# Head products of the second block: from two passes of 128 rows to three passes of 64 rows, two heads by turns

## The chip, the cores and the metric

The kernel runs on one core of a Trainium2 chip, in one launch. The metric is the device time of one execution in microseconds (us), the median of several runs; lower is better. Each core has five engines with instruction streams of their own: PE (TensorE) multiplies matrices, DVE (VectorE) and ACT (ScalarE) work element by element, POOL (GpSimd) does odd jobs, and SP issues most of the transfers. The profile shows PE in two rows: PE for the products themselves, and PEld for the loads of the stationary operand that go ahead of each product.

## What is computed

Two networks run one behind the other on 512 tokens of 1024 channels. Block 1 is a mixer of four branches and a mixture of experts. Block 2, where the change lies, is two layers, each with a token mixer of 16 heads of 64 channels and an MLP:

```python
HEAD_DIM = 64
RET_HEADS = 4      # retention: rotated q and k, decay by distance, chunks of 128
DSA_HEADS = 4      # attention over keys that an index chose
DIL_HEADS = 8      # dilated attention
IDX_HEADS = 8      # heads of the index, 64 channels each; the best keys by their weighted relu scores
...
inner = jnp.einsum('bhncd,bhnmd->bhncm', qc, kc) * decay[None, :, None]
```

All four use products of queries and keys over the 64 channels of one head, which this text calls head products. Float32 accuracy is wanted, and the kernel makes it from parts: a float32 value is split into a high part in the engine's one-pass format (fp32r) and the low part that is left over, and a product of two values is the sum of the products of their parts.

## The kernel before

Everything is traced by `Net`. Its work is written as threads (generators) that yield the engine on which they go on and what they wait for; `run` picks, by a rough clock of the engines (`Clock`), the thread that can start first, and each engine then runs its instructions in the order in which they were picked. No order is written out by hand. `Clock.cost` prices a product by its columns alone.

The activations lie as 128 channels by 512 tokens. `jobs_block2` lists the projections of a layer, and `stream` runs them with their weights loaded ahead; `chan` is one of them: 8 chunks of the contraction in three products each (`mm3`: high by high, high by low, low by high), 512 columns wide. `v_job` makes values, 256 columns wide. While the projections run, the units of the heads are mixed between them: `ret_head` (retention), `idx_unit` (the index), `causal_unit` (the masked attentions of both kinds). Each takes a bank of PSUM (`bank` in the trace, 8 of them, 512 columns each), makes its head product into it, and hands it to DVE or ACT.

A pair of heads comes out of a projection as 128 rows: the first head's 64 channels, then the second's. The kernel before rearranges these for each head, in tiles of the ring `G` (10 tiles of 128 x 1024):

- `stack` puts a head's query parts on top of each other: 64 rows of high parts, 64 rows of low parts. It takes one copy on ACT and one subtraction on DVE, of 64 rows each.
- `dup` writes a head's key parts in both halves of the rows: a copy and a subtraction, and two further copies on ACT or DVE, whichever the clock finds less busy.

With that a head product is two passes over all 128 rows: the stacked queries by the doubled high parts of the keys, then by the doubled low parts. In the code this is the loop `for z in range(2)` in each unit. The three tiles of a pair of heads (`qk_tiles`) are the stacked queries, the keys' high parts and the keys' low parts.

A unit's products are 256, 384 or 512 columns wide (never under 256: narrower ones are made wider). `attend` keeps a number of units under way: 3 of retention, 6 of the masked attentions. In the trace all instructions carry one line, L320, since a helper issues them, so groups go by tiles: `G,G` are the head products, `g_hi`, `g_lo` the activations, `whi`, `wlo` the parts of the weights, `mt` the ring of scratch tiles, `vr` the values, `cP` and `cT` the probabilities and their transposes.

Of the kernel before, what the change touches and what calls it, by code (L numbers as in the profile page):

```python
# [27 lines left out]
F32R = mybir.dt.float32r  # L28
I32 = mybir.dt.int32
AF = mybir.ActivationFunctionType  # L30
OP = mybir.AluOpType
# [171 lines left out]
def _span(ap):  # L203
    """the tile of an access pattern, and the range of its elements on a partition"""
    pairs = ap.ap
    row = pairs[0][0]
    lo = ap.offset % row if row > 0 else ap.offset
    hi = lo
    for s, n in pairs[1:]:
        d = s * (n - 1)  # L210
        if d < 0:
            lo += d
        else:
            hi += d
    return ap.tensor.name, lo, hi + 1


class Clock:
# [91 lines left out]
class Lane:  # L310
    """an engine, with what is traced on it noted on the clock"""
# [26 lines left out]
class Ring:  # L338
    """tiles that are taken and given back in any order"""
# [28 lines left out]
class Net:  # L368
    """The kernel. What it does is written as threads (generators), which yield the engine that their next
    instructions run on and what those wait for; `run` traces them in the order of a rough clock's times, the first  # L370
    in time first. Each engine runs its instructions in the order in which they are traced."""
# [199 lines left out]
    def proj(self, out, w, act, kt, n):  # L571
        """out[128 channels, n tokens] = the weights' columns by the activations"""
# [5 lines left out]
    def proj_t(self, out, w, act, t):  # L578
        """out[128 tokens of tile t, 256 channels]; w: the two halves of the contraction"""
# [7 lines left out]
    def split(self, hi, lo, src, *free):  # L587
        """hi + lo = src; then the rings' tiles in `free` are given back"""
# [7 lines left out]
    def evacuate(self, out, p, n):  # L596
        """a bank's first n columns into out"""
# [8 lines left out]
    def evacuated(self, ring, p, n):  # L606
        """a bank's first n columns, in a tile of the ring"""
# [8 lines left out]
    def rsqrt_mean(self, out, sums, n):  # L616
        """out = (sums / n + eps) ** -0.5"""
# [6 lines left out]
    def row_bcast(self, out_sb, colv, nt):  # L624
        """out_sb[128, nt * 128] = the [128 tokens, nt] column values, along the tokens on every row"""
# [8 lines left out]
    def square(self, acc, x, sq, first, scaled=None):  # L634
        """acc (+)= x ** 2, by a tile of the ring sq; scaled: also (f * x) ** 2, by f and its square"""
# [15 lines left out]
    def column_sums(self, r, acc, nt, n):  # L651
        """r[128 tokens, nt] = (mean over n channels of the squares in acc + eps) ** -0.5"""
# [7 lines left out]
    def sumsq(self, p, nt, k, x, sq):  # L660
        """columns of p: the sums over the 128 channels of chunk k of x ** 2, by tokens"""
# [9 lines left out]
    def rms(self, r, p, nt, nk):  # L671
        """r[128 tokens, nt] = (mean over the chunks' channels + eps) ** -0.5; the bank p is given back"""
# [6 lines left out]
    def square_last(self, x, sq, event):  # L679
        """a tile of the ring sq with x ** 2"""  # L680
# [25 lines left out]
    def silu_c(self):  # L706
        """silu(c) and silu(c_ctx), and their parts"""
# [26 lines left out]
    def mod_job(self, g, kq, w):  # L734
        """rows of the bank: the parts of c by the weights' columns"""
# [35 lines left out]
    def modulated(self, pool, x, nt, v, hi, lo, name):  # L771
        """hi + lo = x / rms * A + B"""
# [34 lines left out]
    def modulation_rest(self, ws, accs):  # L807
        """g1, sh2, sc2, g2: the two 128-column groups of each unit"""
# [45 lines left out]
    def merge(self, n, a, done=0):  # L854
        """some gates ahead of their branches (the first ones may have been done before)"""
# [25 lines left out]
    def branch_job(self, n, d, w):  # L881
        """acc (+)= 2 sigmoid(gate) * (y @ w), by sigmoid(g) = (tanh(g / 2) + 1) / 2"""
# [116 lines left out]
    # -- convolution  # L999
# [10 lines left out]
    def conv_first(self, *ws):  # L1010
        """some units at once, by parts of the contraction"""
# [21 lines left out]
    def conv_tail(self, c, half, p):  # L1033
        """z = a * sigmoid(b), by sigmoid(b) = (tanh(b / 2) + 1) / 2"""
# [29 lines left out]
    def conv_norm(self):  # L1064
        """silu(rms norm), by silu(v) = (tanh(v / 2) + 1) * v / 2"""
# [25 lines left out]
    # -- Fourier  # L1091
# [35 lines left out]
    def dft(self, g, f):  # L1127
        """y = Re(DFT over tokens and channels): the channels' DFT, then its cosines' less its sines' over the tokens"""
# [44 lines left out]
    # -- neighbourhood attention  # L1173
# [3 lines left out]
    def scratch(self, es):  # L1177
        """rows in DRAM: the values of the neighbourhoods, the experts' input by tokens, and their output by blocks"""
# [5 lines left out]
    def zeros(self):  # L1184
        """a row of zeros after the experts' output"""
# [28 lines left out]
    def pair_ring(self, pool, n, shape, name):  # L1214
        """a ring of tiles for high parts, and the tiles of their low parts by the names of those"""
# [48 lines left out]
    def na_values(self):  # L1264
        """for each pair of heads, the values of the four windows of columns and of the context"""
# [64 lines left out]
    def dup(self, hi, lo, src, rows):  # L1330
        """hi, lo [128, n]: the parts of src's 64 rows, in both halves of the partitions"""
# [1844 lines left out]
```

## Time and profile before

| what | value |
|---|---|
| median of 3 runs | 2463.21 us (2459.06 to 2466.94) |
| span of the profiled execution, first to last instruction | 2460.7 us |
| PE busy in it | 2395.9 us, 97% |
| DVE busy, ACT busy | 1675.1 us, 1236.0 us |
| token mixer of block 2, first layer | about 1160 to 1420 us |
| token mixer of block 2, second layer | about 1800 to 2060 us |

The profile gives the span alone for the profiled execution, no time around it. The span is 2.5 us under the median and inside the range of the runs. In the timeline a product's duration runs from its start to the modelled end of its pipeline, so consecutive products overlap: what a product costs its engine is the distance from its start to the next start, called its slot here, and not its duration. Rows of one group that follow each other are merged, with xN behind them; a merged row of N products divided by N gives the slot, if it is taken to the start of the row behind it.

### The profile page before, as it was taken

The numbers are of one execution on the slowest core, as the hardware profiler recorded it, in microseconds if no ns is written. First come the engines' busy times: TensorE is split into PE (matmuls) and PEld (weight loads), VectorE is DVE, ScalarE is ACT, GpSimd is POOL, SyncE is SP. The second block draws the span as 40 slices with busy tenths as digits, with TensorE's granted clock in tenths as the row PEclk, the third lists the DMA queues.
The fourth block names the chain that finished last, engine by engine and source line by source line (L and its number), as shares of the span: only waits on it lengthen the run. The fifth ranks groups of instructions, "written<-read, shape, count | busy, mean of one in ns | idle before, by whom it ended". The sixth has DMA issues, their size and how long they took to land.

```text
span 2460.7 us, 33539 instructions
## 1 busy us (share of the span) xinstructions
PE 2395.9 (97%) x12332; PEld 2011.6 (82%) x12332; DVE 1675.1 (68%) x3144; ACT 1236.0 (50%) x2135; POOL 160.3 (7%) x179
## 2 busy tenths in 40 slices
PE   7999999999997999999999999999999999999998
PEld 3789788889886788887889888888888888888886
DVE  6997577788455989898998753444569976533443
ACT  4433466468342777775537743332443665432333
POOL 3100122100001110002000000000000000000000
PEclk9999999999997999999999999999999999999999
DMA  6223443521363998985121132222232112222221
GB/s 251 97 69 107 134 128 111 170 77 44 99 213 113 351 384 325 353 325 182 64 78 53 44 103 94 94 97 101 95 101 78 53 64 72 95 100 95 94 98 57
DMA packets 104907, 323.79 MB, mean 132 GB/s; under 512 B 12850, under 2 KB 19922, under 8 KB 104612
## 3 DMA queue, kind: packets, MB, share of 16 engines
q1 hardware_dynamic: 91284, 285.40, 33.0%
q0 software_dynamic: 8560, 25.01, 3.5%
q10 hardware_dynamic: 4896, 11.22, 1.2%
q8 instruction: 98, 1.61, 0.3%
q14 instruction: 69, 0.57, 0.1%
HBM read 308.45 MB, written 13.11 MB: 131 GB/s over the span
## 4 chain that ended last, share of the span: by engine, by line
PE 38%; issue 14%; DVE 1%; DMA 0%; ACT 0%; ACTq 0%; POOLq 0%; POOL 0%; DVEq 0%
PE bank L320 38%; DMA mraw<-yg,dest 0%; DVE wlo L320 0%; DVE G L320 0%; DVE cP L320 0%; DVE ym L320 0%; DVE mt L320 0%; DVE m L320 0%; ACTq L320 0%; DVE x L320 0%; DVE o L320 0%; ACT whi L320 0%; POOLq L3172 0%; POOL r L320 0%; DVE nm L320 0%
## 5 line engine op out<-in xcount | busy, mean ns | idle before, releaser
L320 ACT CAST whi<-wraw 128x1024 fp32r<-128x1024 f32 (+1 forms) x321 | 322.1, 1006 | 666.8 <-PE bank L320 633.2
L320 DVE TENSOR_TENSOR wlo<-wraw,whi 128x1024 fp32r<-128x1024 f32 (+1 forms) x321 | 375.4, 1173 | 155.6 <-ACT whi L320 154.8
L320 PE MATMUL bank<-g_hi,whi 128*128 128x512 f32 x992 | 395.9, 399 | 0.0
L320 PE MATMUL bank<-g_hi,wlo 128*128 128x512 f32 x992 | 387.3, 390 | 0.2
L320 PE MATMUL bank<-g_lo,whi 128*128 128x512 f32 x992 | 386.5, 390 | 0.0
L320 PEld LDWEIGHTS bank<-g_hi,wlo 128*128 128x128 f32 x992 | 186.2, 188 | 40.9 <-DVE wlo L320 1.1
L320 PE MATMUL bank<-h_hi,whi 128*128 128x512 f32 x528 | 216.9, 411 | 1.5 <-ACT whi L320 1.5
L320 PEld LDWEIGHTS bank<-g_hi,whi 128*128 128x128 f32 x992 | 186.5, 188 | 37.9 <-issue 1.9
L320 PEld LDWEIGHTS bank<-g_lo,whi 128*128 128x128 f32 x992 | 186.5, 188 | 37.1 <-issue 1.9
L320 PE MATMUL bank<-h_hi,wlo 128*128 128x512 f32 x528 | 209.3, 396 | 1.3 <-DVE wlo L320 1.3
L320 PE MATMUL bank<-h_lo,whi 128*128 128x512 f32 x528 | 208.6, 395 | 1.6 <-DVE h_lo L320 1.6
L320 PE MATMUL bank<-u_hi,whi 128*128 128x512 f32 x512 | 202.4, 395 | 0.0
L320 PE MATMUL bank<-u_hi,wlo 128*128 128x512 f32 x512 | 200.7, 392 | 0.0
L320 PE MATMUL bank<-u_lo,whi 128*128 128x512 f32 x512 | 198.8, 388 | 0.0
L320 DVE SCALAR_TENSOR_TENSOR mu<-bank,rbc 128x512 f32<-128x512 f32 x64 | 44.0, 691 | 161.0 <-PE bank L320 157.4
L320 ACT CAST whi<-mraw 128x1024 fp32r<-128x1024 f32 x101 | 105.7, 1050 | 55.0 <-PE bank L320 25.1
L320 DVE TENSOR_TENSOR wlo<-mraw,whi 128x1024 fp32r<-128x1024 f32 x101 | 121.0, 1218 | 16.5 <-ACT whi L320 14.5
L320 PEld LDWEIGHTS bank<-h_hi,wlo 128*128 128x128 f32 x528 | 100.6, 191 | 24.5 <-DVE wlo L320 2.5
L320 PEld LDWEIGHTS bank<-h_hi,whi 128*128 128x128 f32 x528 | 101.0, 191 | 21.3 <-ACT whi L320 1.9
L320 PEld LDWEIGHTS bank<-h_lo,whi 128*128 128x128 f32 x528 | 100.9, 191 | 19.5 <-DVE h_lo L320 2.1
L320 PEld LDWEIGHTS bank<-u_hi,wlo 128*128 128x128 f32 x512 | 96.1, 188 | 22.5
L320 PEld LDWEIGHTS bank<-u_lo,whi 128*128 128x128 f32 x512 | 96.1, 188 | 21.2
(539 smaller groups left out, 5017.7 us busy)
## 6 DMA issues: line engine op xcount, KB each, us to landing
mraw<-in_wgu SPq DMA_DIRECT2D x106, 512.0 KB
wraw<-in_win SPq DMA_DIRECT2D x102, 512.0 KB
wraw<-in_wdn SPq DMA_DIRECT2D x78, 512.0 KB
wraw<-in_wup SPq DMA_DIRECT2D x64, 512.0 KB
mraw<-in_wdn SPq DMA_DIRECT2D x50, 512.0 KB
mw<-in_wmod SPq DMA_DIRECT2D x64, 256.0 KB
wraw<-in_wout SPq DMA_DIRECT2D x24, 512.0 KB
wraw<-in_wgu SPq DMA_DIRECT2D x22, 512.0 KB
```

The source lines that it names most:

```text
L320: r = f(*args, **kw)
```

## The change

`put_qk` splits the 128 rows of a pair of heads as they are (`split`: one copy on ACT, one subtraction on DVE, all 128 rows), for queries and keys alike, so `stack` and `dup` are no longer called for them; `dup` stays for the index's keys. A pair of heads holds two tiles of `G` in place of three, and the ring has 9 tiles in place of 10. A head product is then three passes of 64 rows (high by high, high by low, low by high), and `head_products` makes those of a pair of heads by turns: first head, second head, in each pass. The first head's operands lie in rows 0 to 63, the second's in rows 64 to 127, and each head has a bank of its own. The units become units of pairs: `ret_pair`, `idx_pair`, `causal_pair`, each of which takes two banks at once; `attend` keeps 2 and 3 of them under way.

```diff
-        self.G = self.ring(pool, 10, [128, 1024], F32R, "G")
+        self.G = self.ring(pool, 9, [128, 1024], F32R, "G")
...
-        self.attend([self.ret_head(L, c, i) for c in range(2) for i in range(2)], 3)
-        u = [self.causal_unit(L, "l", hd, qt) for hd in range(8) for qt in range(4)]
-        u[24:24] = [self.causal_unit(L, "s", hd, qt) for hd in range(4) for qt in range(4)]
-        self.attend(u, 6)
+        self.attend([self.ret_pair(L, c) for c in range(2)], 2)
+        u = [self.causal_pair(L, "l", c, qt) for c in range(4) for qt in range(4)]
+        u[12:12] = [self.causal_pair(L, "s", c, qt) for c in range(2) for qt in range(4)]
+        self.attend(u, 3)
...
-            t = [self.G.take() for _ in range(3)]
+            t = [self.G.take() for _ in range(2)]
...
     def put_qk(self, tiles, j, t):
-        for i in range(2):
-            if j == 0:
-                yield from self.stack(tiles[0][:, i], t, 64 * i)
-            else:
-                yield from self.dup(tiles[1][:, i], tiles[2][:, i], t, 64 * i)
+        yield from self.split(tiles[j][:, 0], tiles[j][:, 1], t)
+
+    def head_products(self, outs, a, b):
+        for z, (y, x) in enumerate(((0, 0), (0, 1), (1, 0))):
+            for i in range(2):
+                r = slice(64 * i, 64 * i + 64)
+                self.nc.tensor.matmul(outs[i], a[y][r], b[x][r], start=z == 0, stop=z == 2)
...
-    def causal_unit(self, L, kind, hd, qt):
+    def causal_pair(self, L, kind, c, qt):
+        nn = max(128 * (qt + 1), 256)
+        yield PE, f"{kind}{L}{c}", (self.banks, 2)
+        q, k = self.D[kind, c][0]
+        ss = [self.banks.take() for _ in range(2)]
+        self.head_products([s[:, :nn] for s in ss], [q[:, z, qt * 128:(qt + 1) * 128] for z in range(2)],
+                           [k[:, z, :nn] for z in range(2)])
+        self.used((kind, c), 4)
+        for i in range(2):
+            self.spawn(self.causal_unit(L, kind, 2 * c + i, qt, ss[i]), 0, "head")
+        yield PE, f"head{L}{kind}{2 * c}{qt}", f"head{L}{kind}{2 * c + 1}{qt}"
+
+    def causal_unit(self, L, kind, hd, qt, s):
```

`ret_pair` and `idx_pair` are changed in the same way.

How PE's instructions stand is shown at two places. The first is in the retention of the first layer of block 2, between the last projections of its gates; `mt,vr` are the retention's products with the values. Before:

```order
L320 MATMUL bank_73<-mt_9636,vr_9646 128x384
L320 MATMUL bank_69<-mt_9637,vr_9646 128x256
L320 MATMUL bank_71<-G_9634,G_9635 128x256
L320 MATMUL bank_71<-G_9634,G_9626 128x256
L320 MATMUL bank_67<-G_9634,G_9635 128x256
L320 MATMUL bank_67<-G_9634,G_9626 128x256
L320 MATMUL bank_66<-g_hi,whi_103 128x512
L320 MATMUL bank_66<-g_lo,whi_103 128x512
```

Now:

```order
L320 MATMUL bank_69<-mt_9636,vr_9645 128x256
L320 MATMUL bank_66<-G_9633,G_9634 128x256
L320 MATMUL bank_68<-G_9633,G_9634 128x256
L320 MATMUL bank_66<-G_9633,G_9634 128x256
L320 MATMUL bank_68<-G_9633,G_9634 128x256
L320 MATMUL bank_66<-G_9633,G_9634 128x256
L320 MATMUL bank_68<-G_9633,G_9634 128x256
L320 MATMUL bank_73<-g_hi,whi_103 128x512
```

Two heads' products were four of 128 rows, a bank after the other; they are six of 64 rows, the banks by turns, with products of 128 rows on both sides. The rows shown (128x256) are those of the output, which stay.

The second place is near the end of the first layer's mixer, in the masked attentions, where transposes (`ident,cP`) and products with the values (`cT,vr`) stand around the head products. Before:

```order
L320 MATMUL bank_66<-cT_9645,vr_9649 128x128 x2
L320 MATMUL bank_67<-G_9630,G_9632 128x256
L320 MATMUL bank_67<-G_9631,G_9632 128x256
L320 MATMUL bank_70<-G_9630,G_9632 128x384
L320 MATMUL bank_70<-G_9631,G_9632 128x384
L320 MATMUL bank_68<-G_9630,G_9632 128x512
L320 MATMUL bank_68<-G_9631,G_9632 128x512
L320 MATMUL bank_73<-ident,cP_9640 128x128 x3
```

Now:

```order
L320 MATMUL bank_66<-cT_9644,vr_9647 128x128 x2
L320 MATMUL bank_70<-G_9631,G_9630 128x512
L320 MATMUL bank_68<-G_9631,G_9630 128x512
L320 MATMUL bank_70<-G_9631,G_9630 128x512
L320 MATMUL bank_68<-G_9631,G_9630 128x512
L320 MATMUL bank_70<-G_9631,G_9630 128x512
L320 MATMUL bank_68<-G_9631,G_9630 128x512
L320 MATMUL bank_69<-ident,cP_9639 128x128 x3
```

Units of three different sizes stood together; now it is one size of one pair. Over both layers there were 352 head products in 79 unbroken runs; there are 528 in 50 runs, 34 of them of one pair (six products), 14 of three pairs, one of four and one of eight.

## Rows read from the trace of the kernel before

**Rows 1.** The page: PE's busy time, and the granted clock in 40 slices.

```profile
PE 2395.9 (97%) x12332; PEld 2011.6 (82%) x12332; DVE 1675.1 (68%) x3144; ACT 1236.0 (50%) x2135; POOL 160.3 (7%) x179
...
PEclk9999999999997999999999999999999999999999
```

**Rows 2.** Busy time by engine in block 2's two token mixers (stretch: length, busy).

```profile
1160.00:1420.00 260.00, 259.12 (x1520) 223.56 (x1519) 227.80 (x593) 156.34 (x327) 7.10 (x6) 1.00 0.19 63
...
1800.00:2060.00 260.00, 259.19 (x1513) 223.10 (x1512) 215.60 (x570) 152.31 (x321) 9.90 (x10) 1.00 0.21 68
```

**Rows 3.** PE's waits from 1160 to 1420 us (waiter, awaited: total us, times).

```profile
PE bank L320 <- DVE cT L320: 0.5, 1, 0.5
PE bank L320 <- DVE mt L320: 0.2, 1, 0.2
```

**Rows 4.** Head products by width, both layers (count, busy us, mean ns, idle).

```profile
L320 PE MATMUL bank<-G,G 128*128 128x256 f32 x160 | 31.7, 304 | 0.0
L320 PE MATMUL bank<-G,G 128*128 128x512 f32 x96 | 29.8, 398 | 0.0
L320 PE MATMUL bank<-G,G 128*128 128x384 f32 x96 | 28.8, 381 | 0.1
```

**Rows 5.** Timeline of PE (start, duration): products 256, 384 and 512 wide.

```profile
1187.37 0.40 PE L320 MATMUL bank<-G,G 128*128 128x256 f32 x2
1187.61 0.29 PE L320 MATMUL bank<-whi,g_hi 128*128 128x256 f32 x1
...
507.05 0.33 PE L320 MATMUL bank<-kd_lo,qs 128*128 128x384 f32 x1
507.22 0.33 PE L320 MATMUL bank<-kd_hi,qs 128*128 128x384 f32 x1
...
1199.27 0.62 PE L320 MATMUL bank<-G,G 128*128 128x512 f32 x2
1199.73 0.28 PE L320 MATMUL bank<-whi,g_hi 128*128 128x256 f32 x1
```

**Rows 6.** Loads of PEld by group: eight at a time, 128 rows and 4 rows.

```profile
L320 PEld LDWEIGHTS bank<-ones,rbc 128*128 128x128 f32 x8 | 1.0, 192 | 0.0
...
L320 PEld LDWEIGHTS bank<-pairs,m 4*128 4x128 f32 x32 | 3.9, 186 | 4.2 <-DVE m L320 2.5 <-issue 1.3 <-DVE A L320 0.4
```

**Rows 7.** Timeline of PE: transposes of 8 rows between products 512 wide.

```profile
1810.63 0.39 PE L320 MATMUL bank<-g_lo,whi 128*128 128x512 f32 x1
1810.86 0.39 PE L320 MATMUL bank<-g_hi,wlo 128*128 128x512 f32 x1
1811.18 0.41 PE L320 MATMUL bank<-ident,mt 8*128 8x8 f32 x4
1811.52 0.50 PE L320 MATMUL bank<-g_hi,whi 128*128 128x512 f32 x1
1811.86 0.40 PE L320 MATMUL bank<-g_lo,whi 128*128 128x512 f32 x1
```

**Rows 8.** Timeline of PE: transposes of 8 rows between products 256 wide.

```profile
1183.52 0.28 PE L320 MATMUL bank<-whi,g_lo 128*128 128x256 f32 x1
1183.73 0.41 PE L320 MATMUL bank<-ident,mt 8*128 8x8 f32 x4
1184.07 0.39 PE L320 MATMUL bank<-whi,g_hi 128*128 128x256 f32 x1
1184.29 0.28 PE L320 MATMUL bank<-wlo,g_hi 128*128 128x256 f32 x1
```

**Rows 9.** Timeline of PEld around the same 8-row transposes at 1811 us.

```profile
1811.17 0.32 PEld L320 LDWEIGHTS bank<-ident,mt 8*128 8x128 f32 x4 [0.35 <-ACT G L320]
1811.52 0.19 PEld L320 LDWEIGHTS bank<-g_hi,whi 128*128 128x128 f32 x1
1811.62 0.19 PEld L320 LDWEIGHTS bank<-g_lo,whi 128*128 128x128 f32 x1
```

**Rows 10.** ACT and DVE groups that write the tiles G, 512 wide.

```profile
L320 ACT CAST G<-mt 64x512 fp32r<-64x512 f32 x50 | 30.8, 616 | 22.2 <-DVE mt L320 21.6
L320 ACT CAST G<-G 64x512 fp32r<-64x512 f32 x34 | 21.0, 619 | 2.4 <-DVE G L320 1.6
...
L320 ACT CAST G<-mt 128x512 fp32r<-128x512 f32 x2 | 1.2, 624 | 0.0
...
L320 DVE TENSOR_TENSOR G<-mt,G 64x512 fp32r<-64x512 f32 x50 | 34.2, 684 | 2.0 <-ACT G L320 0.8
```

More of the change, by code (lines that the diff above doesn't have):

```diff
@@ L2732, in rg_job, with ret_pair @@
         self.mark(f"rg{L}{c}", y)
[L2734 removed]
+    def ret_pair(self, L, c):
         nc = self.nc
[L2736 to L2737 removed]
+        yield PE, f"r{L}{c}", f"v{L}0", (self.banks, 2)
+        q, k = self.D["r", c][0]
         v = self.D["v", 0][0]
[L2739 removed]
+        o = [self.banks.take() for _ in range(2)]
         for b in range(4):
             n, m = 512 - b * 128, max(512 - b * 128, 256)
[L2742 to L2765 removed]
@@ new lines, in ret_pair @@
+            yield PE, (self.banks, 2)
+            ps = [self.banks.take() for _ in range(2)]
+            self.head_products([p[:, :m] for p in ps], [k[:, z, b * 128:(b + 1) * 128] for z in range(2)],
+                               [q[:, z, 512 - m:] for z in range(2)])
+            for i, p in enumerate(ps):
+                yield DVE, p, self.tmp, f"decay{L}{c}"
+                a = self.tmp.take()
+                nc.vector.tensor_tensor(a[:, :n], p[:, m - n:m], self.dec[:, i, :n], op=OP.mult)
+                self.cnt["decay"] = self.cnt.get("decay", 0) + 1
+                self.banks.drop(p)
+                yield PE, a
+                nc.tensor.matmul(o[i][:, 512 - n:], v[:, b, 128 * c:128 * c + 128], a[:, :n], start=b == 0, stop=b == 3)
+                self.tmp.drop(a)
@@ L2767, in ret_norm @@
+        self.used(("r", c), 1)
+        self.used(("v", 0), 2)
+        for i in range(2):
+            yield ACT, o[i], self.tmp if i == 0 else None
+            if i == 0:
+                ot = self.D["ro", c] = self.tmp.take()
+            nc.scalar.copy(ot[64 * i:64 * i + 64], o[i][64 * i:64 * i + 64])
+            self.banks.drop(o[i])
+        self.mark(f"ro{L}{c}", ot)
+        yield from self.ret_norm(L, c)
     def ret_norm(self, L, c):
@@ L2832, in iq_job @@
         g = self.G.take()
-        for i in range(2):
-            yield from self.stack(g[:, 512 * i:512 * i + 384], p[:, 128:], 64 * i)
-            if i:
-                self.banks.drop(p)
-            for qt in (1, 2, 3):
-                self.spawn(self.idx_unit(L, 2 * c + i, qt, g, 512 * i), 1, "idx")
-    def idx_unit(self, L, hd, qt, g, off):
+        yield from self.split(g[:, :384], g[:, 512:896], p[:, 128:], (self.banks, p))
+        for qt in (1, 2, 3):
+            self.spawn(self.idx_pair(L, c, qt, g), 1, "idx")
@@ L2841, in idx_unit, with idx_pair @@
+    def idx_pair(self, L, c, qt, g):
         nc = self.nc
         n = 128 * (qt + 1)
-        yield PE, f"ik{L}", self.banks, g, lambda: hd == 0 or (hd - 1, qt) in self.D
+        yield PE, f"ik{L}", (self.banks, 2), g, lambda: c == 0 or (c - 1, qt) in self.D
         kd, wi, _ = self.D["ik"]
-        s = self.banks.take()
-        for z in range(2):
-            nc.tensor.matmul(s[:, :n], g[:, off + (qt - 1) * 128:off + qt * 128], kd[z][:, :n], start=z == 0, stop=z == 1)
-        yield ACT, s, self.tmp
@@ L2861, in idx_unit @@
-        if self.cnt["i", hd // 2] == 6:
+        ss = [self.banks.take() for _ in range(2)]
+        self.head_products([s[:, :n] for s in ss], [g[:, 512 * z + (qt - 1) * 128:512 * z + qt * 128] for z in range(2)],
+                           [k[:, :n] for k in kd])
+        for i, s in enumerate(ss):
+            hd = 2 * c + i
+            yield ACT, s, self.tmp
+            t = self.tmp.take()
+            nc.scalar.activation(t[:, :n], s[:, :n], AF.Relu)
+            self.banks.drop(s)
+            w, sel = wi[:, qt, hd:hd + 1], self.sel[qt]
+            yield DVE, t
+            if hd == 0:
+                nc.vector.tensor_scalar(sel, t[:, :n], w, None, op0=OP.mult)
+            else:
+                nc.vector.scalar_tensor_tensor(sel, t[:, :n], w, sel, op0=OP.mult, op1=OP.add)
+            self.tmp.drop(t)
@@ L2918, in dq_job @@
         yield PE, f"mix{L}"
[L2919 removed]
+        yield ACT, p, lambda: ("s", c) in self.D or self.G.ready(2) is not None
         yield from self.put_qk(self.qk_tiles(("s", c)), 0, p)
@@ L2969, in lq_job @@
         self.banks.drop(p)
-        yield ACT, t, lambda: ("l", c) in self.D or self.G.ready(3) is not None
+        yield ACT, t, lambda: ("l", c) in self.D or self.G.ready(2) is not None
         yield from self.put_qk(self.qk_tiles(("l", c)), j, t)
@@ L2980, in causal_unit @@
         n = 128 * (qt + 1)
-        nn = max(n, 256)
-        yield PE, f"{kind}{L}{c}", self.banks
-        qs, kh, kl = self.D[kind, c][0]
-        s = self.banks.take()
-        for z in range(2):
-            nc.tensor.matmul(s[:, :nn], qs[:, i, qt * 128:(qt + 1) * 128], (kh, kl)[z][:, i, :nn], start=z == 0, stop=z == 1)
-        self.used((kind, c), 8)
         if kind == "s":
@@ L3022, in causal_unit @@
         self.used(vk, 16)
+        self.mark(f"head{L}{kind}{hd}{qt}")
         self.cnt[key] = self.cnt.get(key, 0) + 1
```

56 lines of the change are left out of this document (10 added, 46 removed).

## The prediction

> **What bounds the kernel now.** I read the page first, for the engine shares and the granted clock. PE is busy 97% of the span at the upper of its two clock levels, 2.4 GHz, nearly throughout [rows 1]. Then the stretches of the two token mixers, since the change lies there: PE is busy 259.1 and 259.2 of 260 us, clock 1.00 in both, while DVE has 228 and 216 us and ACT 156 and 152 [rows 2]. The list of PE's waits confirms it: two waits of 0.5 and 0.2 us in the first mixer [rows 3]. So in this stage no wait ends last; PE's own instructions do. A microsecond added to PE's stream is a microsecond of time, one taken from DVE or ACT is nearly nothing. What I need is the slot of every PE instruction that goes or comes.
>
> **What is removed from PE.** Head products of 128 rows: 160 of 256 columns, 96 of 384, 96 of 512 [rows 4]. Their busy times and means are not slots, since consecutive ones overlap. Slots from start to start [rows 5]: 256 columns (1187.61 - 1187.37) / 2 = 0.12 us; 384 columns 507.22 - 507.05 = 0.17, for which I take 0.175; 512 columns (1199.73 - 1199.27) / 2 = 0.23. The sum is 160 x 0.12 + 96 x 0.175 + 96 x 0.23 = 19.2 + 16.8 + 22.1 = 58.1 us.
>
> **What is added to PE.** The four products of a pair of heads become six of 64 rows: 88 pairs (40 of 256 columns, 24 of 384, 24 of 512), 528 products. No row shows a product of 64 rows, or two products in different halves of the rows, so I bound it from both sides. From below: the halves run wholly side by side, loads included, and a pair of products costs one slot: three slots for a pair of heads in place of four, 58.1 x 3/4 = 43.6 us. From above: nothing runs side by side, six slots in place of four, 58.1 x 6/4 = 87.2 us.
>
> Between these I choose by a floor that the trace does show. Every product reloads its stationary operand. Where the streaming is next to nothing, the loads set the pace: eight loads of 128 columns are busy 1.0 us, (1.0 - 0.192) / 7 = 0.115 us from one to the next; with 4 rows in place of 128 it is 3.9 / 4 groups, (0.975 - 0.186) / 7 = 0.113 [rows 6]. Halving the rows therefore doesn't shorten a load, and no row shows two of them closer than that in this format. I take it that the streams of the two halves overlap, because they use different rows and different banks, and that the loads go one after another at 0.112 us. A pass of two heads then costs the larger of one stream and two loads, 0.224 us: 0.224, 0.224 and 0.23 for the three widths. The sum is 3 x (40 x 0.224 + 24 x 0.224 + 24 x 0.23) = 26.9 + 16.1 + 16.6 = 59.6 us. That is 1.5 us more than what is removed: a narrow group loses (0.67 for 0.48 us), a wide one gains (0.69 for 0.92). In a run of wide products the second head starts one load behind the first and ends that much later, 0.11 us in some 20 runs, 2 us more.
>
> The Trainium skill ("TensorE: Matmul & The Clock Gate", Part 3) says that products in different strips of rows run concurrently, some 4 ns from start to start, 3.07 times faster with four strips. By that rule the sum would be near the lower bound, 43.6 us; no run here shows it yet, and it is the first rival below.
>
> **The changes between 128 and 64 rows.** The trace has a near relative: four transposes of 8 rows between products of 128 rows. Product to product is 0.23 us (1810.63 to 1810.86) [rows 7], but from the last product of 512 columns to the first transpose it is 1811.18 - 1810.86 = 0.32: 0.09 lost. Back again, the first product's duration is 0.50 in place of 0.39, its load begins only with it [rows 9], and the next starts 0.34 behind, 0.11 lost. Behind 256 columns it is the same: 0.21 in place of 0.12 going in, 0.22 in place of 0.12 coming out [rows 8]. From product to product over the transposes 1811.86 - 1810.86 = 1.00 us, of which two slots are 0.46 and four transposes some 0.06 each 0.25: a round trip costs 0.29 us. That is the low end, since the first transpose's load is short. A head product's first load would stand bare for 0.11 like the one coming out: 0.375 us, which I take because its load is of that kind; the high end is 0.09 + 0.11 twice, 0.40. The new order has 50 unbroken runs of head products, so 50 round trips: 50 x 0.375 = 18.8 us (14.5 to 20). The cover for it would be an idle PE, and PE has less than 1 us idle per mixer [rows 2].
>
> These rows are of 8 rows of 128, not of 64. The Trainium skill ("TensorEngine Tiling (Array Packing)", Key Properties) says that any change of tiling mode drains the engine and a change of tile within a mode does not, which would put all 50 runs under the same price and the turns inside a run under none. Without that rule the sum would have 0 here at the least.
>
> **ACT and DVE.** Gone are 64-row copies and subtractions: on ACT 50 + 34 of some 0.62 us, 52 us, beside some 17 us of the narrower or bank-fed ones; instead about 46 of 128 rows at the same price each (0.624 against 0.616 us, since the columns set it) [rows 10]. By the same count ACT and DVE get some 40 us each back. On the path this is nearly nothing: the two mixers' idle PE is 0.9 + 0.8 us [rows 2], plus short stalls under what the view can show. Bounds: -4 us, and +4 us because three pairs under way are less flexible than six heads where the chains through softmax end the mixer. I take 0. The added wait, two banks in place of one and both heads before the next pair, holds up only the unit itself; behind it on PE stand projections that other threads trace. SP, POOL and the transfers are untouched: no step that issues one is moved past another, and the queues carry the same.
>
> **The sum.** -58.1 + 59.6 + 2 + 18.8 + 0 = +22 us. Against the profiled span 2460.7 that is 2483; the median of the runs stands 2.5 us above the span, so I put it on the median: 2463.2 + 22 = **2485 us**.
>
> **The rivals.**
>
> *Streams and loads both overlap.* -58.1 + 43.6 + 18.8 = +4 us, 2467 us, with bounds -3 to +10 from the round trips' and the chains' bounds. For it: separate rows, separate banks. Against it: the loads' spacing, which is the same for 4 rows as for 128.
>
> *Nothing overlaps.* -58.1 + 87.2 + 18.8 = +48 us, 2511 us (2505 to 2515). For it: no row shows two products streaming at once, each starts a whole slot behind the last. Against it: no row has two in different halves either.
>
> *Faster: the round trips are cheap, with streams and loads overlapping.* The gain of three slots for four is 14.5 us. It decides from 14.5 / 50 = 0.29 us per round trip, which is the low end above: if the loads of the other half hide what stands bare when a run begins (0.2 us per round trip, 10 us), and DVE's relief shortens the end of the mixers by 4, the sum is -58.1 + 43.6 + 10 - 4 = -8 us, 2455 us (2449 to 2459). Against it: both 8-row rows show the bare load.
>
> *The change does not do what it says*, that is, the 64-row form is treated like the 128-row one, without halves and without drain: -58.1 + 87.2 = +29 us, 2492 us; it lies within the range.
>
> **How the numbers follow.** The forecast, overlapping streams with loads in turn, 0.35 (+14 to +30); all overlapped 0.30 (-3 to +10); nothing overlapped or the form ignored 0.18 (+29 to +52); faster 0.17 (-14 to -4). A measurement of this kernel tells about 0.3%, 7.4 us, from no change. Faster by more: most of the last case, 0.14. Within: most of the second case, and the ends of others, 0.30. Slower by more: the rest, 0.56. The range reaches from the middle of the faster case, -8, to the middle of the slowest, +49: 2455 to 2512 us, which leaves out less than 2 in 10.
>
> **What would show it.** In the changed trace: (1) six head products of a pair 256 wide, start of the first to start of the last over five: 0.11 says loads in turn, 0.06 all overlapped, 0.12 with full streams nothing overlapped; 512 columns tell more: 0.115 against 0.23 per product. (2) The distance from the last product of 128 rows to the first head product: 0.32 behind 512 columns, not 0.23; and a first product of 128 rows of 0.50 after the run. (3) Some 40 us less busy on ACT and on DVE in the mixers, with PE's waits still under 2 us each. (4) The MLPs and block 1 unchanged. The forecast is wrong if a run's round trip is far from 0.375 us, if two loads do run at once, or if the ends of the mixers show PE waiting for softmax chains.

## The result, and the profile after

The changed kernel takes 2482.3 us (median of 4 runs, 2479.3 to 2484.1) against 2461.8 for the kernel before (4 runs, 2459.1 to 2466.9). The ratio is 1.0083, 95% interval 1.0071 to 1.0095: slower, by 20.5 us. The profiled span is 2481.8 us, 21.1 above the span before. The forecast was 2485 and slower, so the time agrees; the way to it doesn't in two of its steps, and the experiments are mostly about those.

The page of the changed kernel, PE's line and the granted clock, beside [rows 1]:

```profile
PE 2410.3 (97%) x12508; PEld 1996.6 (80%) x12508; DVE 1640.7 (66%) x3067; ACT 1195.5 (48%) x2068; POOL 164.0 (7%) x179
...
PEclk9999999999998999999999999999999999999999
```

ACT is 40.5 us less busy and DVE 34.4. PE has 176 instructions more, is busy 14.4 us longer, and so idles 6.7 us longer than before. Where the time went is found by the time at which the same product of the same projection starts in either trace: 1.1 us are lost before block 2 begins, 11.3 in the first layer's mixer, 8.3 in the second's, nothing in the MLPs. Busy time by stretch (length, then PE, PEld, DVE, ACT, POOL, the granted clock, the share of DMA, GB/s), the two mixers first, then four short stretches of them, beside [rows 2]:

```profile
1160.00:1430.00 270.00, 265.16 (x1600) 215.70 (x1599) 213.41 (x557) 138.08 (x296) 8.01 (x6) 0.99 0.19 61
1810.00:2080.00 270.00, 266.16 (x1607) 216.20 (x1606) 199.69 (x533) 134.10 (x291) 10.81 (x10) 1.00 0.20 67
...
1400.00:1405.00 5.00, 2.73 (x11) 1.76 (x10) 2.83 (x4) 3.21 (x6) 0.00 (x0) 1.00 0.00 0
1405.00:1410.00 5.00, 4.76 (x21) 3.05 (x22) 3.90 (x7) 2.00 (x4) 0.00 (x0) 0.66 0.31 105
...
2055.00:2060.00 5.00, 2.73 (x11) 1.73 (x10) 3.78 (x6) 4.16 (x8) 0.00 (x0) 1.00 0.17 52
2060.00:2065.00 5.00, 4.20 (x29) 2.73 (x28) 4.30 (x16) 1.94 (x8) 0.00 (x0) 1.00 0.15 56
```

A mixer that had 0.8 to 0.9 us of idle PE now has 4.8 and 3.8, and most of it lies in one place of each layer. PE's waits from 1160 to 1430 us (waiter, awaited: total us, times, longest), beside [rows 3]:

```profile
PE bank L320 <- ACT g_hi L320: 1.4, 1, 1.4
PE bank L320 <- DVE g_lo L320: 1.1, 2, 0.8
PE bank L320 <- ACT G L320: 0.7, 1, 0.7
PE bank L320 <- ACT mt L320: 0.5, 1, 0.5
PE bank L320 <- ACT cP L320: 0.4, 2, 0.2
PE bank L320 <- ACT cT L320: 0.3, 1, 0.3
```

The first two are new in kind. The timeline of PE there (start, duration, what; in brackets the idle time before and its releaser):

```profile
1401.59 0.39 PE L320 MATMUL bank<-g_hi,wlo 128*128 128x512 f32 x1
1403.40 0.50 PE L320 MATMUL bank<-g_hi,whi 128*128 128x512 f32 x1 [1.43 <-ACT g_hi L320]
1404.74 0.49 PE L320 MATMUL bank<-g_lo,whi 128*128 128x512 f32 x1 [0.84 <-DVE g_lo L320]
...
1407.75 0.63 PE L320 MATMUL bank<-g_hi,wlo 128*128 128x512 f32 x1
1408.17 0.63 PE L320 MATMUL bank<-g_hi,whi 128*128 128x512 f32 x1
1408.60 0.63 PE L320 MATMUL bank<-g_lo,whi 128*128 128x512 f32 x1
1409.03 0.43 PE L320 MATMUL bank<-g_hi,wlo 128*128 128x512 f32 x1
```

This is the place where the last projection of the mixer ends and the output projection begins (`mixed_job`). The output projection needs the mixers' results split into high and low parts. In the code (`mixed`) these parts are written over the tiles that the projections read, so ACT starts on them only at 1402.74, behind the last projection and a cast of weights, and DVE at 1404.00. For that time PE needs other work, and here it has none: nothing of the attentions stands in the gap. On top of that the granted clock falls from 1.00 to 0.66 over 1405 to 1410 us: from 1407.75 on, products 512 wide start 0.42 us apart, not 0.23, which is the lower of the two levels, 1.2 GHz. Twelve products take 1409.03 - 1401.59 = 7.44 us; at 0.23 us they are 2.7. So 4.7 us are lost here, and 3.9 at the same place of the second layer (6.60 us for twelve products from 2055.64), where the clock stays up.

The head products themselves, by width (count, busy us, mean ns, idle), beside [rows 4]:

```profile
L320 PE MATMUL bank<-G,G 64*128 64x512 f32 x144 | 23.7, 421 | 0.9 <-ACT G L320 0.7
L320 PE MATMUL bank<-G,G 64*128 64x256 f32 x240 | 22.6, 304 | 0.2
L320 PE MATMUL bank<-G,G 64*128 64x384 f32 x144 | 18.1, 346 | 0.6 <-ACT mt L320 0.5
```

A product 512 wide is busy for 23.7 / 144 = 0.165 us of engine time, first loads included, where its own stream needs 0.23: two run at once. The single records say how closely: the two of a pass start 3 to 4 ns apart (1229.403 and 1229.406), and so do their two loads (1229.401 and 1229.404), and the next pass starts 0.115, 0.173 or 0.23 us later by width, the slot of one product. A lone run of six products, entry and exit with it, beside [rows 7, 8]:

```profile
1229.40 0.79 PE L320 MATMUL bank<-G,G 64*128 64x384 f32 x6
1230.12 0.50 PE L320 MATMUL bank<-g_hi,whi 128*128 128x512 f32 x1
1230.46 0.39 PE L320 MATMUL bank<-g_lo,whi 128*128 128x512 f32 x1
...
1877.81 0.39 PE L320 MATMUL bank<-g_hi,wlo 128*128 128x512 f32 x1
1878.13 1.27 PE L320 MATMUL bank<-G,G 64*128 64x512 f32 x6
```

Going in, 1878.13 - 1877.81 = 0.32 us behind a product 512 wide, 0.09 more than its slot; the first pass is followed 0.104 us late, since its load stands bare. Coming out, 0.09 more again from the last pass to the first product of 128 rows, whose duration is 0.50 and behind which the next starts 0.34 later (1230.46 - 1230.12), 0.11 late. Together 0.39 us for a round trip, where the forecast had 0.375.

### The profile page after: what moved, and what is told of

It reads as the page before. It is cut to its first block, busy times and chain, and to the rows that moved or that the text cites. A ratio compares the mean times of both kernels' runs of the same rounds, so it can differ in the third digit from the quotient of the medians.

```text
span 2481.8 us, 33723 instructions
## 1 busy us (share of the span) xinstructions
PE 2410.3 (97%) x12508; PEld 1996.6 (80%) x12508; DVE 1640.7 (66%) x3067; ACT 1195.5 (48%) x2068; POOL 164.0 (7%) x179
## 4 chain that ended last, share of the span: by engine, by line
PE 69%; issue 15%; DVE 7%; ACT 2%; DMA 2%; SPq 0%; another core or an unknown queue 0%; POOL 0%; ACTq 0%; POOLq 0%; DVEq 0%
PE bank L320 69%; DVE wlo L320 1%; DVE sel L320 1%; DMA nbm<-in_rpb 1%; DVE m L320 1%; ACT cP L320 1%; ACT nP L320 0%; SPq L320 0%; DVE macc L320 0%; DVE mt L320 0%; DMA mw<-in_wmod 0%; ACT whi L320 0%; DMA mraw<-yg,dest 0%; DVE g_lo L320 0%
## 5 line engine op out<-in xcount | busy, mean ns | idle before, releaser
L320 PE MATMUL bank<-g_hi,whi 128*128 128x512 f32 x992 | 402.4, 406 | 2.9 <-ACT g_hi L320 2.9
L320 PEld LDWEIGHTS bank<-h_hi,whi 128*128 128x128 f32 x528 | 100.9, 191 | 21.1 <-ACT whi L320 1.9
```

What stands on the lines that cost most here:

```text
L320: r = f(*args, **kw)
```

## The experiments

Two theories stood at first. By the forecast's, passes are set by the loads in turn, 59.6 us for the 528 products, and a round trip costs 0.375. By its first rival, streams and loads both overlap, 43.6 us, and what is missing to the measured time is waits that the new order makes. The records above speak for the second; the runs ask what each piece is worth to the whole. Unless another base is named, an edit is against the changed kernel.

**Without the turns.** The six products are issued head by head.

```diff
-        for z, (y, x) in enumerate(((0, 0), (0, 1), (1, 0))):
-            for i in range(2):
+        for i in range(2):
+            for z, (y, x) in enumerate(((0, 0), (0, 1), (1, 0))):
```

> The changed kernel with its six head products of a pair in another order: the first head's three passes, then the second head's, in place of turns. Nothing else is edited. Theory (the two halves of the array work side by side, streams and loads alike, when consecutive products lie in different halves): only the last pass of the first head can overlap the first of the second, so a pair costs five slots in place of three; in sum 58.1 x 5/4 = 72.6 us in place of 43.6, so about 29 us over the changed kernel, near 2511 us; products of one head start a whole slot apart (0.12 to 0.23 us) and not 0.003. Rival (loads go in turn, as the prediction had it): 72.6 in place of 59.6, 13 us over, near 2495 us. Rival (nothing overlaps): no difference, 2482 us.

Measured: 2487.8 us, 1.0108 of the kernel before (1.0090 to 1.0127), 5.4 above the changed kernel. No theory had that; the two that counted on an overlap thought that the second head would stand behind the first. The timeline of PE at a lone run of this kernel, of the same width as the one above:

```profile
1226.68 0.80 PE L320 MATMUL bank<-G,G 64*128 64x384 f32 x6
1227.40 0.50 PE L320 MATMUL bank<-g_hi,whi 128*128 128x512 f32 x1
```

Six products take 0.80 us against 0.79 by turns. Their records start in twos, 10 ns apart (1226.677 and 1226.687, 1226.958 and 1226.968, 1227.132 and 1227.142), and the last two are those that signal the end of a head: the second head's first product does not wait for the first head's third. Most of the 48 runs of this kernel go like that. So the turns are hardly needed for the overlap. Where the 5.4 us lie, the traces say in part: PE waits for ACT cP, the probabilities, 3.2 and 3.3 us in the two mixers, where the changed kernel has 0.4 and 0.2, and the runs take 46.2 us from first to last product, not 43.2. Why this order makes those waits isn't shown.

**A product of zeros of 128 rows** in each group of six, adding nothing to a bank: once between the first pass and the second, and once behind the third.

```diff
         for z, (y, x) in enumerate(((0, 0), (0, 1), (1, 0))):
+            if z == 1:
+                self.nc.tensor.matmul(outs[0], self.zero[:, :128], self.zero[:, :outs[0].free_size()], start=False, stop=False)
```

> The changed kernel with one more product in each of the 88 pairs: 128 rows of zeros by zeros, of the pair's width, added onto the first head's bank between the first and the second pass. It splits nearly every run of 64-row products: 137 runs in place of 50. Theory (each run of 64-row products between products of 128 rows costs a round trip of about 0.39 us): 88 slots, 40 x 0.12 + 24 x 0.175 + 24 x 0.23 = 14.5 us, and 87 more round trips, 34 us: 48 us over the changed kernel, near 2531 us. Rival (changing between 64 and 128 rows is nearly free, and the loss lies in the waits at the mixers' ends): 14.5 us over, 2497 us.

```diff
-                self.nc.tensor.matmul(outs[i], a[y][r], b[x][r], start=z == 0, stop=z == 2)
+                self.nc.tensor.matmul(outs[i], a[y][r], b[x][r], start=z == 0, stop=z == 2 and i == 1)
+        self.nc.tensor.matmul(outs[0], self.zero[:, :128], self.zero[:, :outs[0].free_size()], start=False, stop=True)
```

> The same product of zeros as in the run beside it, but behind the last pass of each pair, where it ends the accumulation: 88 runs of 64-row products. The work is the same, 49 runs fewer. Theory (round trips): 14.5 us of slots and 38 round trips of 0.39, 15 us: 29 us over the changed kernel, near 2512 us, and 19 us under the run with the zeros inside. Rival (changes are free): 14.5 us over, and no difference between the two.

Measured: inside 2519.0 us, 1.0234 (1.0219 to 1.0250), 36.7 above the changed kernel; behind 2504.3, 1.0172 (1.0157 to 1.0188), 22.0 above. The two differ by 49 runs of products of 64 rows (137 against 88) and by nothing else in PE's work, and PE's listed waits in the mixers are nearly the same, 5.2 and 4.8 us: 14.7 us, 0.30 each. A change of row count and back therefore costs the whole kernel some 0.30 us or more; without such a price they would be equal. Both are some 7 to 12 us below what records would give (behind: 14.5 us of products and 38 round trips of 0.39 are 29), and some 3 of them are waits that the added work covers: the changed kernel's listed waits are 7.9 us. The doubling below shows the same.

**Every pass twice.** The six products are issued a second time over, into the same banks with the same operands.

```diff
                 self.nc.tensor.matmul(outs[i], a[y][r], b[x][r], start=z == 0, stop=z == 2)
+        off, self.clk.off = self.clk.off, True
+        for z, (y, x) in enumerate(((0, 0), (0, 1), (1, 0))):
+            for i in range(2):
+                r = slice(64 * i, 64 * i + 64)
+                self.nc.tensor.matmul(outs[i], a[y][r], b[x][r], start=z == 0, stop=z == 2)
+        self.clk.off = off
```

> Each group of six products of 64 rows is issued twice over, the second time into the same banks with the same operands, so the output stays; the order of everything else and the 50 runs stay. So 528 products are added and no change between row counts. If both the streams and the loads of the two halves overlap, each added pass costs one slot: 3 x (40 x 0.115 + 24 x 0.173 + 24 x 0.23) = 13.8 + 12.5 + 16.6 = +42.8 us over the changed kernel, some 2525 us, and 2 to 5 less if it fills part of the waits at the change to the output projection. If loads went in turn, as the prediction took it: +59.6 us, 2542. If nothing overlapped: +87, 2569.

Measured: 2513.4 us, 1.0212 (1.0196 to 1.0228), 31.1 above the changed kernel; by the spans 32.6. The head products of this kernel by width:

```profile
L320 PE MATMUL bank<-G,G 64*128 64x512 f32 x288 | 39.2, 404 | 0.0
L320 PE MATMUL bank<-G,G 64*128 64x256 f32 x480 | 36.3, 290 | 0.0
L320 PE MATMUL bank<-G,G 64*128 64x384 f32 x288 | 29.8, 338 | 0.0
```

For 256 columns 36.3 - 22.6 = 13.7 us more for 120 added passes, 0.114 each; loads in turn would need 0.224. For 512 it is (39.2 - 23.7) / 72 = 0.215. In all the stretches from the first to the last product of the runs grow by 40.3 us (43.2 to 83.5), near the 42.8 expected, and 19 below loads in turn. Of these 40.3 the kernel pays 31 to 33: the added work covers waits that were open, and in this trace the waits for G, mt, cP and cT are gone from the list. So added work under-measures here; the price of a product is taken from its slot, and the waits have to be found by themselves.

**One part at a time,** each on the kernel before: the index, the retention, the masked attentions. Of the first the edit's core is

```diff
-            for qt in (1, 2, 3):
-                self.spawn(self.idx_unit(L, 2 * c + i, qt, g, 512 * i), 1, "idx")
+        for qt in (1, 2, 3):
+            self.spawn(self.idx_pair(L, c, qt, g), 1, "idx")
```

> The kernel before with the change made in the index alone (its queries kept as 128-row parts, head products in 3 passes of 64 rows by turns); retention and masked attention as before, 10 tiles of G. 6 runs of 64-row products, of 18 to 48. Theory (halves side by side, 0.39 us per run): 8 times one slot of each width saved, 8 x (0.12 + 0.175 + 0.23) = 4.2 us, less 6 x 0.39 = 2.3: 1.9 us under the kernel before, 2459 us, at most 4 us worse if products inside the runs wait for ACT's scratch tiles. Rival (64-row products cost time whatever the runs' length): 3 us or more over the kernel before.

of the second

```diff
-        self.attend([self.ret_head(L, c, i) for c in range(2) for i in range(2)], 3)
+        self.attend([self.ret_pair(L, c) for c in range(2)], 2)
```

> The kernel before with the change made in the retention alone: 16 runs of 6 products. Theory: 4 pairs of heads save a slot of 512, 384 and twice 256 columns each, 4 x 0.645 = 2.6 us; 16 round trips of 0.39 cost 6.2: 3.7 us over the kernel before, 2465 us. Rival (changes between row counts are free): 2.6 us under it.

and of the third the lines of `causal_pair` and `attend(u, 3)` of the change.

> The kernel before with the change made in the masked attentions alone (units of pairs, three under way): 28 runs of 64-row products. Theory: 12 pairs of heads save 12 x 0.645 = 7.7 us, 28 round trips cost 10.9, and the wait between the last projection and the output projection, some 4 us per layer, comes with the units of pairs: 11 us over the kernel before, 2473 us. Rival (that wait comes from elsewhere, the retention or the index): 3 us over it, 2465 us.

Measured against the kernel before: index 1.0014 (1.0005 to 1.0023), +3.5 us; retention 1.0015 (1.0006 to 1.0024), +4.4; masked attentions 1.0064 (1.0052 to 1.0077), +16.6. The three add up to 24.5, the whole is 20.5. The retention is as worked out: 16 runs, a price of 3.7. The index should have gained 1.9, and its 3.5 is what the rival had; but the rival's reason, that products of 64 rows cost time whatever the runs' length, doesn't agree with the doubling. In its trace PE waits 1.2 us for ACT mt, the scratch tiles for which the theory allowed up to 4, and its span is only 0.6 us above that of before; the rest isn't assigned. The masked attentions were to cost 3 by slots and round trips and 11 with the hole; they cost 16.6, and their waits say where most of it lies. PE's waits from 1160 to 1430 us with the masked attentions alone:

```profile
PE bank L320 <- DVE g_lo L320: 1.6, 2, 0.8
PE bank L320 <- ACT g_hi L320: 1.4, 1, 1.4
```

They are the waits of the changed kernel at the same place, where twelve products take 6.6 us again (from 1398.23), 3.9 lost in each layer. The index alone and the retention alone have no wait for g_hi or g_lo. So the hole in front of the output projection comes with the change of the masked units, which stand last in the mixer.

**Two ways to fill the hole.** First, the last pair of the masked attentions is held back until the projections are done, so that something is left to issue:

```diff
-        yield PE, f"{kind}{L}{c}", (self.banks, 2)
+        yield PE, f"{kind}{L}{c}", (self.banks, 2), f"projected{L}" if kind == "s" and c == 1 and qt > 1 else None
```

> The changed kernel, in which the two widest units of the last pair of the index-chosen attention in each layer wait until the last projection is under way to its end (the event that starts the output projection). Nothing else is edited; 52 runs of 64-row products in place of 50. Theory (some 4 us per layer of the loss is PE waiting between the last projection and the output projection, for the copies that make the parts of the mixers' output, since the units of heads have run dry there): the held units cover that wait, 4 to 9 us under the changed kernel, 2473 to 2478 us. Rival (that wait has another cause, or moves to the end of the mixer): within 2 us of the changed kernel or above it.

Second, a unit issues two sizes of its pair one behind the other, with four banks, and two units are under way, not three (37 runs of products of 64 rows, not 50):

```diff
-        u = [self.causal_pair(L, "l", c, qt) for c in range(4) for qt in range(4)]
+        u = [self.causal_pair(L, "l", c, qts) for c in range(4) for qts in ((0, 1), (2, 3))]
...
-        self.attend(u, 3)
+        self.attend(u, 2)
...
-        yield PE, f"{kind}{L}{c}", (self.banks, 2)
+        yield PE, f"{kind}{L}{c}", (self.banks, 4)
```

> The changed kernel with two sizes of a pair's queries in one unit of the masked attentions (four banks taken at once, 12 products in a row, two units under way in place of three): 37 runs of 64-row products in place of 50, the same 528 products. Theory (the runs carry the cost): 13 round trips fewer, 5 us under the changed kernel, 2477 us, if four banks at once hold nothing up. Rival (runs are no cost): no less than the changed kernel.

Measured: held 2479.0 us, 1.0072 (1.0058 to 1.0086), 3.3 below the changed kernel; two sizes 2479.1, 1.0072 (1.0060 to 1.0084), 3.2 below, a little less than the theories had (4 to 9, and 5). Each trades one wait for another. PE's largest wait from 1160 to 1430 us, of the kernel with held units and of that with two sizes:

```profile
PE bank L320 <- DVE g_lo L320: 2.2, 1, 2.2
```

```profile
PE bank L320 <- ACT cP L320: 4.1, 5, 1.1
```

With 13 runs fewer, 5 us of round trips went in the second, and the waits for g_hi and g_lo fell to 1.8 us in each layer; but waits for the softmax came, 4.1 us in this mixer and 4.5 in the other.

**The price in the planner.** The order is traced by a rough clock of the engines, which prices a product of 64 rows like one of 128, as if the two heads' products ran one after the other. Here one of 64 rows is put at half; nothing else is edited.

```diff
-            k = int(t / 3.4133)
+            n, k = n / (2 if ins[0].partition_size() == 64 and ins[0].dtype == F32R else 1), int(t / 3.4133)
```

> The clock that sets the order while tracing counts a product of 64 rows at half its price, which is nearer to what the pair of them takes; nothing else is edited, so only the order of the work changes (54 runs of products of 64 rows in place of 50, 1.6 us more). Theory: the two waits at the change to the output projection (7.4 and 6.6 us where 2.7 us of work is done) come from an order laid out by wrong prices, and shrink: 3 to 6 us less than the changed kernel, 2476 to 2479. Rival: they come from units that bind two heads and two banks to each other, whatever the price, so that nothing is left to fill the last chains: within 2 us of the changed kernel, 2480 to 2484, with the same waits for g_hi and g_lo.

Measured: 2469.9 us (5 runs, 2466.4 to 2470.9), 1.0035 (1.0021 to 1.0048): 12.4 below the changed kernel, twice the most that the theory had, and 9.6 above the kernel before. PE's waits from 1160 to 1430 us, all of them, and the timeline of PE where the last projection ends (1393.10) and the output projection begins (1397.12):

```profile
PE bank L320 <- ACT cT L320: 0.7, 1, 0.7
PE bank L320 <- DVE g_lo L320: 0.5, 2, 0.2
PE bank L320 <- DVE G L320: 0.4, 2, 0.3
PE bank L320 <- ACT g_hi L320: 0.2, 1, 0.2
```

```profile
1393.10 0.39 PE L320 MATMUL bank<-g_hi,wlo 128*128 128x512 f32 x1
1393.33 1.72 PE L320 MATMUL bank<-cT,vr 128*128 128x128 f32 x14
1394.89 0.60 PE L320 MATMUL bank<-ident,cP 128*128 128x128 f32 x4
1396.20 1.16 PE L320 MATMUL bank<-cT,vr 128*128 128x128 f32 x8 [0.71 <-ACT cT L320]
1397.12 0.48 PE L320 MATMUL bank<-g_hi,whi 128*128 128x512 f32 x1
```

The hole is gone but for waits of 0.2 us, and with it the fall of the clock, 1.00 throughout from 1390 to 1410 us: transposes and products with the values now stand between the last projection and the output projection, and ACT has begun with the parts at 1396.05. The same two-head units, bound to the same two banks, issue without it, so the rival of this run falls: the hole came from the order, not from the units. The span is 7.4 us above that of before; 54 round trips of 0.39 less 14.5 saved are 6.6. By the medians it is 9.6, and the listed waits of the two mixers, 1.8 and 1.4 us against 0.7 and 0.5 of the kernel before, are 2 of the 3 between. In this kernel slots and round trips make most of the sum. That it takes the right price to get such an order isn't shown: one order was compared with one other.

**Fewer round trips at that price.** First, all pairs in halves, in 37 runs: masked units with two sizes, and the retention with two blocks of keys at once.

```diff
-        for b in range(4):
+        for b0 in (0, 2):
...
-            yield PE, (self.banks, 2)
+            yield PE, (self.banks, 4)
```

> The half price of the run before, and longer unbroken runs: a masked unit issues two sizes of its pair one behind the other (four banks, two units under way in place of three), and the retention issues two of its four blocks of keys at once. All 88 pairs stay in halves, in 37 runs of products of 64 rows in place of 50. Theory (three slots for four save 14.5 us, a change of row count and back costs 0.39 us, no other price): 37 x 0.39 - 14.5 = 0 against the kernel before, 2460 to 2462. Rival: units of four banks wait for their own chains, as they did with the old price: +5 to +10, 2466 to 2471.

Second, the two sizes for the masked units and the index as changed, with the retention left as before the change.

```diff
-        self.attend([self.ret_pair(L, c) for c in range(2)], 2)
+        self.attend([self.ret_head(L, c, i) for c in range(2) for i in range(2)], 3)
```

> Only the index and the masked attentions take the form in halves, the masked units with two sizes at once, at the half price; the retention stays as it was before the change, head by head in products of 128 rows. 72 pairs (32 of 256 columns, 20 of 384, 20 of 512) save 32 x 0.12 + 20 x 0.175 + 20 x 0.23 = 11.9 us; 28 runs cost 28 x 0.39 = 10.9. Theory: -1 us against the kernel before, 2458 to 2461; with the lower price of a round trip by whole kernels (0.30) it would be -3.5, 2457. Rival: the waits of units with four banks: +4 to +8, 2464 to 2469.

Measured: long runs 2464.6 us, 1.0016 (1.0007 to 1.0025), 3.3 above the kernel before; index and masked attentions 2465.0, 1.0018 (1.0009 to 1.0027), 3.6 above. The theory had 0 and -1, the rival 5 to 10 and 4 to 8. PE's waits from 1160 to 1430 us in the kernel with long runs (the second layer's read the same):

```profile
PE bank L320 <- DVE g_lo L320: 1.3, 2, 0.8
PE bank L320 <- ACT g_hi L320: 0.5, 1, 0.5
```

1.8 us in each layer, 3.6 in all against the 1.2 of the kernel before, which is most of the 3.3 that are missing. So 37 runs pay for their round trips with what the halves save, and the waits of the four-bank units at the output projection are left over. These are the same as in the kernel with two sizes at the old price, which has 37 runs too and takes 14.5 us longer; what is gone are its 4.1 and 4.5 us of waits for the softmax. So the price seems worth about as much there, and not by the hole; the retention's form differs as well, so this is not shown by itself. No version that was run beats the kernel before.

## Why the prediction came out right

**What is removed, and the bound.** Confirmed. PE was full in the mixers, the MLPs and block 1 are unchanged, and everything happens in the two mixers.

**What is added: this step was wrong.** It chose loads in turn, 59.6 us, from the spacing of loads of 128 and of 4 rows [rows 6]. Those rows show that fewer rows don't shorten a load, which is still so (0.10 us of a bare first load); they say nothing on two loads in different halves, and these start 3 to 4 ns apart. Three slots in place of four, 43.6 us: the step was 16 us too dear, and the 2 us of skew with it. The rival *streams and loads both overlap* had the mechanism. The Trainium skill ("TensorE: Matmul & The Clock Gate", Part 3) has some 4 ns from start to start for products in different strips, and the trace agrees with 3 to 4.

**The round trips.** Right, for the reason given: 50 x 0.39 = 19.5 us against 18.8, with three of the four pieces as the 8-row transposes had shown them, and the fourth, the bare first load, as the forecast had added it (0.104 us). Measured between whole kernels it is 0.30. The Trainium skill ("TensorEngine Tiling (Array Packing)", Key Properties) says that a change of mode drains the engine and a change of tile within it does not; the price at the ends of a run, and none at the turns inside, agree.

**ACT and DVE, and the waits: wrong by its size, and by its reason.** The step took 0, with bounds of 4 us either way. ACT and DVE gave back 40.5 and 34.4 us, as worked out, and no gain from it shows in the time. But the waits of the new order cost far more than 4: 8.6 us at the two output projections (4.7 and 3.9), 2.8 in stalls inside the runs (some 1.5 of them in the index's two runs of the first layer, at passes that wait for ACT, and most of the rest where a second or third pass stands for an operand's low part), and some 2 in other listed waits. The step's reason for its upper bound was that three pairs under way are less flexible than six heads; with the planner's price halved the same three pairs leave no hole. It also counted on projections to stand behind a waiting unit, and behind the last projection there are none. No single wait is over 2 us, as the forecast said they wouldn't be; it should have asked for their sum, and for what stands behind them: at the first output projection a wait of 1.4 and one of 0.8 cost 4.7, with the fall of the clock that came with them.

**The sum.** 43.6 - 58.1 + 19.5 + 8.6 + 2.8 + 2 = +18.4 us, less the 1.2 us of waits that the kernel before had in the two mixers: some 17 of the measured 20.5. Of the rest 1.1 arose before block 2, and some 2 aren't assigned. The forecast's +22 was right by luck: a term 16 to 18 us too dear stood beside one some 13 us too cheap. Of the signs of being wrong that it named, one came, two loads that run at once; at the ends of the mixers PE waits too, but for the operands of the output projection more than for the softmax. The best evidence is the run with the planner's price: without the hole the kernel comes at +9.6 us, at the upper end of the rival's -3 to +10 and not in the forecast's own +14 to +30.

**What the diff had shown.** The order rows ahead of the prediction showed that the order around the head products changes, and the forecast read off them only the runs and their number. The clock in the kernel prices a product by its columns alone, whatever its rows, and the change leaves that as it is: a pair of heads that takes three slots is planned as six. That could have been read in `cost` beforehand. Nor has the clock a price for the 0.39 us of a run, at the old price or at the half; what an order planned with it would be worth, no run tells.

**Left open.** Why PE waits longer for the softmax without the turns; what the index alone loses besides 1.2 us of waits; and some 3 us of the masked attentions alone, whose slots, round trips and waits explain 13 of 16.6.

## What to carry to other kernels

Splitting TensorE's rows in halves pays by the length of an unbroken run: a pair of heads saves one slot (0.12 to 0.23 us here), and every run pays 0.39 us once, so that a lone group of six loses and two to four of them only break even. Where a kernel's order is planned from prices, a change of an instruction's form is also a change of its price, and the planner has to be told: here that was worth 12 of the 20 us lost, in the one order that was run. And a total that comes out right proves none of its terms: check each against its own rows.

## What the runs showed of the hardware

Two loads of TensorE in different halves of the rows run side by side like the products, 3 to 4 ns from start to start. A change from products of 128 rows to products of 64 and back costs 0.39 us by the records: 0.09 going in, 0.10 for the bare first load, 0.09 coming out and 0.11 behind the first product of 128 rows. The halves need not be served by turns: with one head's three products issued ahead of the other's, the other's first started 10 ns behind the one's first (1226.677 and 1226.687), ahead of products that were issued before it. A wait of the same kind and length took the granted clock down in one layer (PE busy 2.73 of 5 us, then 0.66 over the next 5) and not in the other (2.73 of 5, then 1.00); what else decides it no run here tells.
